# An RWKV-7 layer whose triangular inverses are turned on chip, with their lower products moved into the receptance projection

## The chip, the cores and the metric

The kernel runs on one core of one Trainium2 chip. The metric is the device time of one execution in microseconds (us), lower being better. All times below are in us unless another unit is given. The engines are TensorE (PE; its weight loads are listed as PEld), VectorE (DVE), ScalarE (ACT), GpSimd (POOL) and SyncE (SP, which here only issues DMAs).

## What is computed

Two residual layers run on 512 tokens of width 2048, in float32. Layer 0 is differential attention, and nothing of it concerns this study. Layer 1 is RWKV-7: projections to receptance r, key k, value v and gate g, a per-channel decay, and a recurrence per head of 64 channels (32 heads), followed by a normalisation per head, the gate and an output projection.

```python
p = h @ w_in                      # r, k, v, gate: 2048 columns each, and two low-rank parts
p = p + (token_shift(p) - p) * mu
...
kk = kk / max(norm(kk), 1e-12)    # per head
def step(S, inp):                 # S: 64 x 64 per head
    r_t, w_t, k_t, v_t, a_t, b_t = inp
    sa = einsum('bhvk,bhk->bhv', S, a_t)
    S = S * w_t[:, :, None, :] + sa[..., None] * b_t[:, :, None, :] + v_t[..., None] * k_t[:, :, None, :]
    y = einsum('bhvk,bhk->bhv', S, r_t)
    return S, y
```

Here a_t is -kk, and b_t is kk times a learned rate.

## The kernel before

**Pairs and chunks.** Layer 1 works through 16 pairs of heads, j = 0 to 15, of 128 channels each. The 512 steps of the recurrence are cut into eight chunks of 64. Within a chunk the recurrence is a triangular system, so the kernel computes for each chunk and head the inverse of a unit lower triangular 64x64 matrix, and with it runs a scan over eight chunks in place of 512 steps.

**Projections.** A projection of one pair (`unit_chan`) is 48 matmuls of 128x512 into the tile pp (L129): 16 slices of the 2048 inputs, each with three products. ACT casts the weights to a high part (wh, L115), and DVE subtracts to get the low part (wl, L116). Both have four buffers, so these two engines keep a little ahead of TensorE. Pair by pair the order is v(j), k(j+1), gate(j-3), r(j+1); the first three pairs have no gate.

**One pair's way.** After r(j), `stage2` completes the tile AR. Behind the 18th matmul of v(j), `gram` multiplies BK by AR per chunk and head (tile gp, L1091). ACT copies the result to G (L1098), and two matmuls (L1010, L1011) sum k squared per head, for the norm. The two 32x32 diagonal blocks of each triangular matrix (16 per half, 32 in all) go by six DMAs on ACT's queue to DRAM (ltd), and come back by four DMAs on POOL's queue as LT, one matrix per partition and repeated four times, so that each group of 32 partitions solves a quarter of the columns. `t_solve` then runs 31 steps on DVE, each with one L1155 (tmpl) and one L1157 (Tm), and a product with the norm (L1158). POOL's queue writes Tm to DRAM (td), and four DMAs on SP's queue read it into TT, the inverse's diagonal blocks. DVE transposes the upper ones into T1 (L1181). The lower left block of the inverse is minus a product of three: TensorE multiplies G's lower block by T1 (px, L1187, 16 matmuls of 32x32), ACT copies to X (L1190), TensorE multiplies X by TT's lower blocks (px, L1197), and ACT copies into TT (L1200). Both px groups do one head's eight chunks first and the other's behind them.

**The scan.** `scan_pair` does per chunk: sm<-VS,G (L1268); ACT copies to rhs (L1271); sm<-rhs,TT (L1279); ACT copies to VS (L1281); sm<-VS,BKT (L1286); DVE makes the next state (L1290). POOL's copies L1274 and L1277 stand beside it. `others` hangs transposes on TensorE at given chunks: keys (L1130) at 0 and 1, values (L1222) at 2, the finished y of pair j-2 (L1347) at 3. After the last chunk come the outputs Y (L1308, L1312) and their centring.

**What sets the order.** The scan is a generator (`Chain`) that counts projection matmuls: `tick` steps it when as many have passed as its last `yield` said. `t_combine` is the first part of the same chain. Its first step runs with the previous pair's gram, and the px groups follow after GAP_D 18 and GAP_X 19 matmuls; the scan's steps follow after GAP_T 8 with gaps (6, 8) in full pairs, (4, 5) or (3, 4) in the others. The solve has a higher scheduling priority than the scan, and the scan a higher one than the weights. Decays, queries and keys of pair j+1 (`stage1`, L1040 to L1062: the prefix l, its middle m, the exponentials E, and BK) are hung behind the scan's state steps.

Of the kernel before, what the change touches and what calls it, by code (L numbers as in the profile page):

```python
# [23 lines left out]
P = 128  # L24
# [178 lines left out]
def load_rows(g, pieces, rows, queue=None, t=None):  # L203
# [693 lines left out]
def unit_chan(g, parts, cols, step=P, more=None, behind=(0, None), pts=None):  # L897

    nc = g.nc
    n = cols // step  # L900
    pts = pts or [g.pp.tile([P, 512], F32, name="pp", tag="pp") for _ in range(n)]
    KG = 8 if cols == P else 4
    m = None
    for k0 in range(0, KT, KG):
        wh, wl = split_w(g, parts, KG, cols, k0)
        for k, c in [(k, c) for k in range(KG) for c in range(n)]:
            s = slice(c * step, (c + 1) * step)
            kk = k0 + k
            if more and c == 0:
# [3 lines left out]
            if n == 1 and 3 * kk + 3 == behind[0]:  # L913
                behind[1](m)
    return pts
# [12 lines left out]
C = 64  # L928
# [8 lines left out]
def rwkv_consts(g, aps):  # L937
# [10 lines left out]
    pb = load_rows(g, pbs, 112, t=tb)  # L948
# [28 lines left out]
def rwkv_masks(g):  # L977
# [102 lines left out]
def gram(g, j, p, before):  # L1080
# [3 lines left out]
    p.BKT = w.tile([P, NC_, P], F32, name="BKT", tag="BKT", bufs=2)  # L1084
# [8 lines left out]
    if before:  # L1093
        with g.tc.issue_after(m.ins):
            before.step(g)
    for c0, gp in halves:
        for h in range(2):
            nc.scalar.copy(p.G[:, c0 : c0 + 4, :, h, :], gp[h][:].rearrange("p (u x t) -> p u x t", u=4, x=2))  # L1098
    ps = g.ps.tile([P, 512], F32, name="pt", tag="pb", bufs=2)
    sum_channels(g, ps[:2, :], g.ones[:, 0 : P : C], p.k2)  # L1100
    ss = w.tile([2, T], F32, name="ssl", tag="thg", bufs=1)
    nc.scalar.copy(ss[:], ps[:2, :])
    for half in range(2):
        nc.scalar.dma_start(
            out=g.ltd[j % 2, half, :, :, HALF, :],
            in_=ss[:].rearrange("h (c b t) -> h c b t", c=NC_, b=2)[:, :, half, :])
    for half in range(2):
        for h in range(2):
            q0 = h * C + half * HALF
            nc.scalar.dma_start(  # L1110
                out=g.ltd[j % 2, half, h, :, 0:HALF].rearrange("c s t -> s c t"),
                in_=p.G[q0 : q0 + HALF, :, 0, h, half * HALF : (half + 1) * HALF])
# [22 lines left out]
def t_solve(g, j, p):  # L1135
# [4 lines left out]
    LT = w.tile([P, HALF + 1, HALF], F32, name="LT", tag="LT", bufs=1)  # L1140
# [4 lines left out]
    n2 = LT[:, HALF, :]  # L1145
    nc.vector.tensor_scalar(n2, n2, 1e-24, None, ALU.max)
    nc.vector.reciprocal(n2, n2)
    nc.gpsimd.memset(Tm[:], 0.0)
    tf = Tm[:].rearrange("p q t -> p (q t)")
    for i in range(NG):  # L1150
        nc.gpsimd.memset(tf[i * 32 : i * 32 + 32, i :: HALF + NG], 1.0)
# [7 lines left out]
    nc.gpsimd.dma_start(out=g.td[j % 2].rearrange("q l t -> l q t"), in_=Tm[:])  # L1159
    return ld.ins  # L1160


GAP_D, GAP_X, GAP_T = 18, 19, 8


def t_combine(g, j, p):

    nc, w, TT = g.nc, g.work, g.TT[j % 2]
    for h in range(2):
        for half in range(2):  # L1170
            o, l0 = half * HALF, half * 16 + h * NC_
            nc.sync.dma_start(
                out=TT[h * C + o : h * C + o + HALF, :, h, o : o + HALF],
                in_=g.td[j % 2].rearrange("q (g l) t -> (q g) l t", g=NG)[:, l0 : l0 + NC_, :])
    T1 = w.tile([P, NC_, HALF], F32, name="T1", tag="T1", bufs=1)
    X = w.tile([P, NC_, HALF], F32, name="X", tag="X", bufs=1)
    px = g.ps.tile([P, 512], F32, name="px", tag="pd", bufs=1)
    for h in range(2):
        r_ = slice(h * C, h * C + C)
        with g.tc.issue_after(g.centred) if g.centred else ExitStack():  # L1180
            nc.vector.transpose(T1[r_], TT[r_, :, h, 0:HALF])  # L1181
    yield GAP_D
    N = NC_ * HALF
    blocks = [(h, h * C, slice(h * C, h * C + HALF), slice(h * C + HALF, h * C + C)) for h in range(2)]
    for h, b0, lo, hi in blocks:
        for c in range(NC_):
            nc.tensor.matmul(px[hi, c * HALF : (c + 1) * HALF], p.G[lo, c, 0, h, HALF:C], T1[lo, c, :],  # L1187
                             start=True, stop=True, tile_position=(b0, b0 + HALF))
    for _, _, _, hi in blocks:
        nc.scalar.copy(X[hi], px[hi, :N].rearrange("p (c s) -> p c s", c=NC_))  # L1190
    for h, b0, _, _ in blocks:
        r_ = slice(b0, b0 + C)
        nc.scalar.copy(p.G[r_, :, 0, h, :], p.AR[r_, :, 0, :])
    yield GAP_X
    for h, b0, lo, hi in blocks:
        for c in range(NC_):
            nc.tensor.matmul(px[lo, N + c * HALF : N + (c + 1) * HALF], X[hi, c, :], TT[hi, c, h, HALF:C],  # L1197
                             start=True, stop=True, tile_position=(b0 + HALF, b0))
    for h, b0, lo, _ in blocks:
        nc.scalar.copy(TT[lo, :, h, HALF:C], px[lo, N:].rearrange("p (c s) -> p c s", c=NC_))  # L1200
    yield GAP_T
# [46 lines left out]
def chain(g, j, p, delay, gap, gap_s, others=()):  # L1248
    def steps():
        yield from t_combine(g, j, p)  # L1250
# [65 lines left out]
def centre(g, p):  # L1316
# [4 lines left out]
    for h in range(2):  # L1321
# [3 lines left out]
        c = nc.vector.tensor_sub(p.yc[:, h::2, :], yg, s1[:, :, h : h + 1].to_broadcast([P, NT, C]))  # L1325
    g.centred = c.ins
# [25 lines left out]
def layer1(g, aps):  # L1352
    nc, tc = g.nc, g.tc
    with ExitStack() as cx:
# [18 lines left out]
        def receptances(j):  # L1373
            return shift_mix(g, proj(0, j), P, *mus(g, 0, j), "r", 1)
# [3 lines left out]
        for j in range(D // P):  # L1378
            p = pairs[j]
            if j:  # L1380
                others = [(0, lambda p=p: turn_keys(g, p, 0)), (1, lambda p=p: turn_keys(g, p, 4)),
                          (2, lambda p=p: turn_values(g, p))]
                if j > 1:
                    others.append((3, lambda i=j - 2: finish_y(g, i, pairs[i])))
                full = LAG <= j < D // P - 1
                gaps = (6, 8) if full else (4, 5) if j > 1 else (3, 4)
                chain(g, j - 1, pairs[j - 1], 5, *gaps, others).step(g)
                if j == 1:
                    pairs[0].chain.wait += 28
            stage2(g, j, r, p)  # L1390

            def behind(m, j=j, p=p):
                if j > 1:
                    pairs[j - 2].chain.finish(g)
                with tc.issue_after(m.ins):
                    gram(g, j, p, j > 1 and pairs[j - 1].chain)
                mask_gram(g, p, 0)
                loaded = t_solve(g, j, p)
                with tc.issue_after(loaded):
                    mask_gram(g, p, 1)  # L1400
# [3 lines left out]
            stage_v(g, j, p, proj(2, j, behind=(18, behind)))  # L1404
# [10 lines left out]
        chain(g, j, p, 66, 5, 6)  # L1415
# [10 lines left out]
        gts.append(gate(g, j, proj(3, j, behind=(24, last_but_one)), "E"))  # L1426
# [66 lines left out]
def body(ctx, tc, nc, aps):  # L1493
    g = Ctx()
    g.nc, g.tc = nc, tc
    g.last, g.first, g.centred = None, [], None
# [11 lines left out]
    g.ltd = dr.tile([2, 2, 2, NC_, HALF + 1, HALF], F32, name="ltd")  # L1508
    g.td = dr.tile([2, HALF // NG, P, HALF], F32, name="td")
# [27 lines left out]
```

## Time and profile before

| | us |
|---|---|
| device time, median of 3 runs | 2198.23 |
| lowest and highest run | 2197.27, 2201.91 |
| profiled execution, first to last instruction (span) | 2193.6 |
| TensorE busy in it | 2161.4 |
| DVE busy | 1469.2 |
| ACT busy | 1095.1 |
| POOL busy | 302.0 |
| mean granted TensorE clock | 0.997 |

The profile gives no separate device time for the profiled execution; its span is 4.6 below the median of the runs, and that much lies around the first and last instruction. In the rows below, a group line has line, engine, operation, output and inputs, shape, count, then busy time and mean ns of one, then the idle time of the engine ahead of them and what ended it. A window row has the stretch in us from the start, its length, the busy time and count of each engine, the granted clock (1.00 is full speed), the DMA engines' busy share and GB/s. A wait row has the engine and line that waited, what it waited for, and the total, number and longest. One TensorE matmul of 32-bit data appears as two records.

### The profile page before, as it was taken

To read this page: it belongs to the slowest core of one execution; us is meant where nothing else is said; L and a number is where in the kernel's file an instruction comes from. 1 tells how busy PE (TensorE), PEld (TensorE's weight loads), DVE (VectorE), ACT (ScalarE), POOL (GpSimd) and SP (SyncE) were. 2 spreads that over 40 slices of the span, in tenths; PEclk is the share of its full clock that TensorE was granted. 3 is DMA by queue.
4 is the path that set the end of the run, shared out by engine and by line. 5 is a ranking of instruction groups with operands and counts; after the bars stand their busy time and mean duration, and the time that the engine had idled before them with its cause. 6 is when DMAs were issued, how large, how long until landed. Compare 5 with 4: busy or idle time off the path is not lost.

```text
span 2193.6 us, 35117 instructions
## 1 busy us (share of the span) xinstructions
PE 2161.4 (99%) x12260; PEld 1766.8 (81%) x12260; DVE 1469.2 (67%) x4121; ACT 1095.1 (50%) x2459; POOL 302.0 (14%) x637
## 2 busy tenths in 40 slices
PE   9999999999999999999999999999999999999999
PEld 8888888888888878878777788887888888777887
DVE  5665646465665667476667877777778877767645
ACT  6443434344443454345455566555555566555433
POOL 0000000000000000110223222222222222221001
PEclk9999999999999999999999999999999999999999
DMA  7323222222222356553422333333333333455556
GB/s 193 96 80 99 85 96 97 87 97 87 93 81 97 128 170 231 149 131 89 101 60 73 90 89 85 94 98 92 92 82 90 94 92 79 105 132 188 173 166 122
DMA packets 296321, 240.26 MB, mean 110 GB/s; under 512 B 47792, under 2 KB 255680, under 8 KB 296144
## 3 DMA queue, kind: packets, MB, share of 16 engines
q1 hardware_dynamic: 256912, 190.13, 29.3%
q0 software_dynamic: 12384, 29.72, 6.4%
q10 hardware_dynamic: 26848, 18.18, 2.7%
q8 instruction: 96, 1.57, 0.3%
q14 instruction: 81, 0.66, 0.1%
HBM read 217.98 MB, written 19.99 MB: 108 GB/s over the span
## 4 chain that ended last, share of the span: by engine, by line
PE 80%; DVE 12%; DMA 3%; ACT 3%; issue 2%; POOL 0%; ACTq 0%; DVEq 0%; SPq 0%; POOLq 0%
PE pp L129 60%; PE pt L129 5%; DVE tmpl L1155 2%; DVE wl L116 2%; DVE Tm L1157 1%; PE gp L1091 1%; PE sm L1268 1%; DMA yr<-yd 1%; PE o L129 1%; PE sc L129 1%; DMA td<-Tm 1%; PE sm L1286 1%; PE lora L129 1%; PE sm L1279 1%; DMA TT<-td 1%
## 5 line engine op out<-in xcount | busy, mean ns | idle before, releaser
L116 DVE TENSOR_TENSOR wl<-wraw,wh 128x512 fp32r<-128x512 f32 (+1 forms) x636 | 436.3, 689 | 442.2 <-ACT wh L115 429.7
L115 ACT CAST wh<-wraw 128x512 fp32r<-128x512 f32 (+1 forms) x636 | 393.3, 620 | 589.7 <-PE pp L129 484.4
L129 PE MATMUL pp<-wh,hH 128*128 128x512 f32 x1268 | 499.8, 394 | 0.6 <-DVE prmin_rw_mu_dram L210 0.6
L129 PE MATMUL pp<-wh,hL 128*128 128x512 f32 x1268 | 497.5, 393 | 0.0
L129 PE MATMUL pp<-wl,hH 128*128 128x512 f32 x1268 | 497.4, 392 | 0.0
L129 PE MATMUL pp<-hH,wl 128*128 128x512 f32 x1024 | 414.9, 405 | 0.0
L129 PE MATMUL pp<-hL,wh 128*128 128x512 f32 x1024 | 414.9, 405 | 0.0
L129 PE MATMUL pp<-hH,wh 128*128 128x512 f32 x1024 | 410.8, 401 | 0.0
L129 PEld LDWEIGHTS pp<-wh,hH 128*128 128x128 f32 x1268 | 238.3, 188 | 48.6 <-issue 1.3
L129 PEld LDWEIGHTS pp<-wh,hL 128*128 128x128 f32 x1268 | 238.3, 188 | 48.2
L129 PEld LDWEIGHTS pp<-wl,hH 128*128 128x128 f32 x1268 | 238.3, 188 | 47.1
L129 PEld LDWEIGHTS pp<-hH,wh 128*128 128x128 f32 x1024 | 193.9, 189 | 35.3 <-issue 0.9
L129 PEld LDWEIGHTS pp<-hL,wh 128*128 128x128 f32 x1024 | 193.9, 189 | 34.8
L129 PEld LDWEIGHTS pp<-hH,wl 128*128 128x128 f32 x1024 | 194.0, 189 | 32.4
L1155 DVE SCALAR_TENSOR_TENSOR tmpl<-LT,Tm 128x60 f32<-128x60 f32 (+24 forms) x496 | 133.9, 270 | 11.2
L1274 POOL COPY SA<-VS 64x64 f32<-64x64 f32 x224 | 62.0, 277 | 443.3 <-DVE VS L1290 361.7
L476 POOL DMA_DIRECT2D frow<-yd x12 | 8.9, 746 | 795.9 <-DVE rs_t L67 675.6
L1157 DVE TENSOR_TENSOR Tm<-Tm,tmpl 128x60 f32<-128x60 f32 (+24 forms) x496 | 102.4, 206 | 8.1
L1281 ACT COPY VS<-sm 64x64 f32<-64x64 f32 x256 | 52.9, 207 | 60.5 <-PE sm L1279 50.9
L1271 ACT COPY rhs<-sm 64x64 f32<-64x64 f32 x256 | 52.7, 206 | 60.5 <-PE sm L1268 56.6
L1277 POOL TENSOR_SCALAR Sg<-SA,gam 128x64 f32<-128x64 f32 x96 | 70.2, 731 | 9.5
L1290 DVE SCALAR_TENSOR_TENSOR VS<-sm,gam,Sg 64x64 f32<-64x64 f32 x192 | 54.1, 282 | 19.4 <-PE sm L1286 14.4
(333 smaller groups left out, 3197.9 us busy)
## 6 DMA issues: line engine op xcount, KB each, us to landing
wraw<-in_rw_w_in_dram SPq DMA_DIRECT2D x128, 512.0 KB
wraw<-in_da_w_in_dram SPq DMA_DIRECT2D x254, 256.0 KB
wraw<-in_da_w_out_dram SPq DMA_DIRECT2D x26, 512.0 KB
wraw<-in_rw_w_out_dram SPq DMA_DIRECT2D x26, 512.0 KB
LT<-ltd POOLq DMA_DIRECT2D x64, 132.0 KB, 3.0
yr<-yd SPq DMA_DIRECT2D x28, 256.0 KB
frow<-yd POOLq DMA_DIRECT2D x12, 512.0 KB, 6.5
xq<-in_x_dram SPq DMA_DIRECT2D x16, 256.0 KB
```

Source lines behind the costliest of these rows:

```text
L115: nc.scalar.copy(hi[:], raw[:, k : k + n])
L116: nc.vector.tensor_sub(lo[:], raw[:, k : k + n], hi[:].bitcast(F32))
L129: m = nc.tensor.matmul(out, a, b, start=s, stop=e, skip_group_check=skip)
L1091: m = nc.tensor.matmul(gp[h][:, i * P : (i + 1) * P], BK[r_, c0 + i, :, :], p.AR[r_, c0 + i, :, :], start=True, stop=True)
L1155: nc.vector.scalar_tensor_tensor(tt, LT[:, i : i + 1, i + 1 :].to_broadcast([P, s, n]), n2[:, i : i + 1], Tm[:, 0:s, i : i + 1].to_broadca ...
L1157: nc.vector.tensor_add(Tm[:, 0:s, i + 1 :], Tm[:, 0:s, i + 1 :], tt)
L1268: nc.tensor.matmul(sm[:, 0:P], both(p.G[:, c, 0]), both(VS[:, c]), start=True, stop=True)
L1271: nc.scalar.copy(rhs[r_, :], sm[r_, h * C : h * C + C])
L1274: nc.gpsimd.tensor_copy(p.SA[r_, c - 1, :], VS[r_, c, h, :])
L1277: nc.gpsimd.tensor_scalar(Sg[:], p.SA[:, c - 1, :], p.gam[:, c : c + 1], None, ALU.mult)
L1281: nc.scalar.copy(VS[r_, c, h, :], sm[r_, P : P + C])
L1290: g.state = nc.vector.scalar_tensor_tensor(VS[r_, c + 1, h, :], s_, p.gam[r_, c : c + 1], Sg[r_, :], ALU.mult, ALU.add)
```

## The change

The inverse's blocks no longer pass through DRAM, and the lower products and the norms are put in other places.

- ACT copies the diagonal blocks of G to a tile LP (four copies of 32x256), and one transpose on DVE makes LT from it, four times repeated. Tm starts as a copy of a constant (`unit`), made by POOL once. After the 31 steps and the product, two transposes on DVE make T1 and W, and POOL copies W into TT's diagonal blocks. The tiles ltd and td are gone.
- The norms are summed in the receptance projection of the same pair, behind its 24th matmul (`norms`), and three DMAs on POOL's queue take them through a small DRAM tile nd to n2.
- The px groups of pair j-1 become `t_first` and `t_second`, behind the 9th and 33rd matmul of r(j), with the two heads alternating. Only for the last pair do they still run in the chain (`whole`).
- The scan's chain of pair j-1 starts with r(j) done, after 3 matmuls, with gaps (7, 8) in full pairs, (5, 6) for j below 3 and (4, 5) for j = 15. The transposes of values move from chunk 2 to 4, those of y from 3 to 5.
- Both halves of the mask on G are issued before the solve. The order of T1 behind the centring is gone. One parameter tile moves from the const pool to a temporary one.

```diff
 def gram(g, j, p):
...
+    p.LP = w.tile([P, NC_, HALF], F32, name="LP", tag="tmpl", bufs=1)
+    for h in range(2):
+        for half in range(2):
+            q = slice(h * C + half * HALF, h * C + half * HALF + HALF)
+            nc.scalar.copy(p.LP[q], p.G[q, :, 0, h, half * HALF : (half + 1) * HALF])
+def norms(g, j, p, m):
...
+    with g.tc.issue_after(m.ins):
+        sum_channels(g, ps[:2, :], g.ones[:, 0 : P : C], p.k2)
...
 def t_solve(g, j, p):
...
+    nc.vector.transpose(LT[:].rearrange("p (r c) t -> p t r c", r=NG),
+                        p.LP[:].rearrange("p c t -> p t c")[:, :, None, :].to_broadcast([P, HALF, NG, NC_]))
...
-    for i in range(NG):
-        ld = nc.gpsimd.dma_start(out=LT[i * 32 : i * 32 + 32], in_=g.ltd[j % 2].rearrange("b h c s t -> (b h c) s t"))
...
+    nc.gpsimd.tensor_copy(Tm[:], g.unit[:])
...
-    nc.gpsimd.dma_start(out=g.td[j % 2].rearrange("q l t -> l q t"), in_=Tm[:])
...
+    nc.vector.transpose(p.T1[:].rearrange("p c (q r) -> p q r c", r=NG),
+                        Tm[:].rearrange("p q (r c) -> p q r c", r=NG))
+    p.W = w.tile([P, NC_, HALF], F32, name="W", tag="Tm", bufs=1)
+    nc.vector.transpose(p.W[:], p.T1[:])
...
+            nc.gpsimd.tensor_copy(g.TT[j % 2][q, :, h, o : o + HALF], p.W[q])
...
+def t_first(g, j, p):
...
+    for c in range(NC_):
+        for h, b0, lo, hi in BLOCKS:
+            nc.tensor.matmul(px[hi, c * HALF : (c + 1) * HALF], p.G[lo, c, 0, h, HALF:C], p.T1[lo, c, :],
                              start=True, stop=True, tile_position=(b0, b0 + HALF))
...
+def t_second(g, j, p):
...
+    for c in range(NC_):
+        for h, b0, lo, hi in BLOCKS:
+            nc.tensor.matmul(px[lo, N + c * HALF : N + (c + 1) * HALF], p.X[hi, c, :], p.W[hi, c, :],
                              start=True, stop=True, tile_position=(b0 + HALF, b0))
...
+            behind = [(24, lambda m: norms(g, j, pairs[j], m))]
+            if j:
+                behind += [(9, piece(t_first, j - 1, pairs[j - 1])), (33, piece(t_second, j - 1, pairs[j - 1]))]
+            return shift_mix(g, proj(0, j, behind=behind), P, *mus(g, 0, j), "r", 1)
...
-                gaps = (6, 8) if full else (4, 5) if j > 1 else (3, 4)
-                chain(g, j - 1, pairs[j - 1], 5, *gaps, others).step(g)
-                if j == 1:
-                    pairs[0].chain.wait += 28
+                gaps = (7, 8) if full else (5, 6) if j < LAG else (4, 5)
+                chain(g, j - 1, pairs[j - 1], 3, *gaps, others)
```

Three places show how the order moves. The first is TensorE in a full pair. Before, around the gram in v(j), the px groups stand together beside the gram (G and T are those of pair j-1, gp and the sums pt those of pair j):

```order
L129 MATMUL pp<-hL,wh 128x512
L129 MATMUL pp<-hH,wl 128x512
L1187 MATMUL px<-T_14796,G_14131 32x32 x8
L1091 MATMUL gp<-AR,BK 128x128 x2
L1187 MATMUL px<-T_14796,G_14131 32x32 x8
L1091 MATMUL gp<-AR,BK 128x128 x14
L1197 MATMUL px<-TT_10025,X 32x32 x16
L1010 MATMUL pt<-sHx,ones 2x512
L1011 MATMUL pt<-sLx,ones 2x512
L129 MATMUL pp<-hH,wh 128x512
```

Now, in r(j), the second px group stands behind the outputs of the pair before and the norms' sums, and the first stands 24 projection matmuls ahead of it, alone (not in these rows):

```order
L129 MATMUL pp<-hH,wl 128x512
L1328 MATMUL Y<-VS,G_14881 64x64 x16
L1332 MATMUL Y<-SA,AR 64x64 x14
L1019 MATMUL pt<-sHx,ones 2x512
L1020 MATMUL pt<-sLx,ones 2x512
L129 MATMUL pp<-hH,wh 128x512
L129 MATMUL pp<-hL,wh 128x512
L129 MATMUL pp<-hH,wl 128x512
L129 MATMUL pp<-hH,wh 128x512
L129 MATMUL pp<-hL,wh 128x512
L129 MATMUL pp<-hH,wl 128x512
L1211 MATMUL px<-W,X 32x32 x16
```

So px left v, and the gram stands there without it. The second place is ACT in the k projection, where the scan's rhs and VS of one pair meet the decays (m, l, E) and BK of the next. Before:

```order
L1054 ACTIVATE BK<-th_15229,prm_bk_b_1234,prm_bk_s_1231 128x8x64
L1271 COPY rhs<-sm 64x64 x2
L115 CAST wh<-wraw 128x512
L1044 ACTIVATE E<-m 128x8
L1045 ACTIVATE E<-l 128x8x64
L1281 COPY VS<-sm 64x64 x2
L1046 ACTIVATE l<-l 128x512
```

Now:

```order
L115 CAST wh<-wraw 128x512
L1053 ACTIVATE E<-m 128x8
L1063 ACTIVATE BK<-th_15215,prm_bk_b_1233,prm_bk_s_1230 128x8x64
L1291 COPY rhs<-sm 64x64 x2
L1054 ACTIVATE E<-l 128x8x64
L1055 ACTIVATE l<-l 128x512
L1301 COPY VS<-sm 64x64 x2
```

E<-m moved ahead of rhs. What it reads comes from DVE, whose rows at the same place were, before, in the middle of the solve:

```order
L1157 TENSOR_TENSOR Tm<-Tm,tmpl 128x3x22
L1040 SCALAR_TENSOR_TENSOR l<-rmask,th_15223 128x512
L1155 SCALAR_TENSOR_TENSOR tmpl<-LT,Tm 128x63
L1042 TENSOR_SCALAR m<-l 128x8
L1157 TENSOR_TENSOR Tm<-Tm,tmpl 128x3x21
L1043 TENSOR_TENSOR l<-l,m 128x512
L1155 SCALAR_TENSOR_TENSOR tmpl<-LT,Tm 128x60
```

And now:

```order
L1169 SCALAR_TENSOR_TENSOR tmpl<-LT,n_15449,Tm 128x8
L1049 SCALAR_TENSOR_TENSOR l<-rmask,th_15926 128x512
L1171 TENSOR_TENSOR Tm<-Tm,tmpl 128x8
L1051 TENSOR_SCALAR m<-l 128x8
L1172 TENSOR_TENSOR Tm<-Tm,n_15449 128x256
L1052 TENSOR_TENSOR l<-l,m 128x512
L1174 STREAM_TRANSPOSE T_15702<-Tm 128x32x8
```

The scan for l and m moved from the solve's 11th step to its last, because the solve starts earlier against the projections.

The third place is TensorE at pair 0, in r(1), where the built order puts t_first behind 31 projection matmuls of r(1), and the norms' sums and t_second right behind it:

```order
L129 MATMUL pp<-hH,wh 128x512
L1196 MATMUL px<-T_10382,G_10278 32x32 x16
L1019 MATMUL pt<-sHx,ones 2x512
L129 MATMUL pp<-hL,wh 128x512
L129 MATMUL pp<-hH,wl 128x512
L129 MATMUL pp<-hH,wh 128x512
L129 MATMUL pp<-hL,wh 128x512
L129 MATMUL pp<-hH,wl 128x512
L1211 MATMUL px<-W,X 32x32 x16
L129 MATMUL pp<-hH,wh 128x512
```

In the order before, r(1) holds no px; px of pair 0 comes in v(1), beside the gram.

More of the change, by code (lines that the diff above doesn't have):

```diff
@@ L912, in unit_chan @@
                     kk == 0, kk == KT - 1, g)
-            if n == 1 and 3 * kk + 3 == behind[0]:
-                behind[1](m)
+            for at, follow in behind:
+                if 3 * kk + 3 == at:
+                    follow(m)
     return pts
@@ L1177, in t_combine @@
[L1177 to L1182, printed above, removed]
+            o = half * HALF
+            q = slice(h * C + o, h * C + o + HALF)
+            nc.gpsimd.tensor_copy(g.TT[j % 2][q, :, h, o : o + HALF], p.W[q])
+BLOCKS = [(h, h * C, slice(h * C, h * C + HALF), slice(h * C + HALF, h * C + C)) for h in range(2)]
@@ L1495, in body @@
     g.nc, g.tc = nc, tc
[L1496 removed]
+    g.last, g.first = None, []
     g.chains, g.later, g.state = [], [], None
```

128 lines of the change are left out of this document (61 added, 67 removed).

## Prediction

> **What bounds the kernel now.** I read the page's engine totals and its chain first, then the stretches from one gram (L1091) to the next, then what TensorE waits for. The first two lines come from the page.
>
> ```profile
> PE 2161.4 (99%) x12260; PEld 1766.8 (81%) x12260; DVE 1469.2 (67%) x4121; ACT 1095.1 (50%) x2459; POOL 302.0 (14%) x637
> PE 80%; DVE 12%; DMA 3%; ACT 3%; issue 2%; POOL 0%; ACTq 0%; DVEq 0%; SPq 0%; POOLq 0%
> ```
>
> TensorE is busy nearly always, so an edit pays only where it shortens TensorE's own work or one of its few stops. Layer 0 keeps its order. Layer 1 I cut at the gram's start: the first row is pair 0's gram to pair 1's, then pairs 1, 2 and 3, ten pairs in one row, pair 14, and the rest. After the range and its length come the busy times of PE, PEld, DVE, ACT and POOL, the granted clock and the DMAs.
>
> ```profile
> 1038.13:1076.98 38.85, 38.84 (x200) 31.51 (x199) 24.32 (x63) 21.96 (x41) 5.90 (x10) 1.00 0.36 90
> 1076.98:1140.59 63.61, 57.96 (x369) 44.13 (x368) 44.38 (x136) 31.76 (x79) 15.81 (x36) 0.89 0.30 75
> 1140.59:1196.33 55.74, 53.54 (x374) 39.89 (x373) 41.80 (x133) 32.43 (x80) 17.52 (x36) 1.00 0.27 67
> 1196.33:1263.29 66.96, 64.03 (x453) 49.70 (x452) 51.71 (x154) 36.31 (x87) 17.52 (x42) 1.00 0.37 95
> 1263.29:1877.92 614.63, 607.95 (x4187) 497.35 (x4185) 474.38 (x1379) 358.77 (x860) 159.46 (x360) 1.00 0.35 90
> 1877.92:1941.46 63.54, 61.59 (x440) 50.38 (x437) 48.32 (x139) 36.22 (x86) 15.95 (x36) 1.00 0.44 118
> 1941.46:2193.60 252.14, 246.73 (x1325) 198.19 (x1322) 153.68 (x333) 106.74 (x225) 40.38 (x67) 1.00 0.56 157
> ```
>
> A steady pair takes 614.63/10 = 61.46. Pairs 1 and 2 lack a gate projection, 48 matmuls. The chain gives their price:
>
> ```profile
> 1062.08 14.96 PE pp L129 x66
> ```
>
> That is 0.2267 each, so 10.9 for 48, and pairs 1 and 2 should take about 50.5. Pair 1 is 13.1 over, pair 2 is 5.2, pair 3 is 5.5, pair 14 is 2.1. That excess is what there is to win. Its cause is in the waits of PE, and for pair 1 in the chain and in windows around the longest wait:
>
> ```profile
> PE px L1187 <- DVE T L1181: 10.4, 9, 4.5
> PE sm L1268 <- DVE VS L1290: 4.8, 14, 0.6
> PE sm L1279 <- ACT rhs L1271: 1.1, 2, 0.7
> ```
>
> ```profile
> 1087.57 0.43 DVE Tm L1158
> 1088.29 3.23 DMA td<-Tm
> 1091.67 1.74 DMA TT<-td
> 1093.43 0.45 DVE T L1181
> ```
>
> ```profile
> 1089.00:1093.90 4.90, 0.39 (x2) 0.00 (x0) 1.93 (x5) 0.59 (x1) 2.04 (x9) 0.92 0.52 126
> 1093.90:1106.30 12.40, 12.38 (x86) 9.63 (x86) 2.37 (x4) 3.72 (x9) 2.68 (x4) 0.50 0.48 111
> 1203.70:1206.20 2.50, 0.96 (x6) 0.48 (x4) 0.43 (x2) 0.59 (x1) 0.75 (x5) 1.00 0.30 48
> ```
>
> At px of pair 0, TensorE stood 4.5 for the inverse's way through DRAM, and then ran 12.4 at half clock, which lost about 6 more. The stop in pair 3 (2.50 − 0.96, about 1.5) did not do that: pair 3's whole stretch has 1.00.
>
> **The change, part by part.** *Early pairs.* The way from Tm to T1 (1087.57 to 1093.88, 6.3) becomes Tm's product and one transpose, about 0.9, and the loading of LT through DRAM becomes four copies on ACT and a transpose on DVE. But px of pair 0 now stands behind the 31st matmul of r(1), some 25 earlier. TensorE gets there at about 1062.1 − 0.5 (the norms' two sums have moved) + 31 × 0.2267 = 1068.6. The other side of that race:
>
> ```profile
> 1039.32 2.05 ACT L1098 COPY G<-gp 128x512 f32<-128x512 f32 x4 [2.05 <-PE gp L1091]
> 1059.08 0.24 DVE L1155 SCALAR_TENSOR_TENSOR tmpl<-LT,Tm 128x31 f32<-128x31 f32 x1
> L115 ACT CAST wh<-wraw 128x512 fp32r<-128x512 f32 x160 | 99.3, 621 | 112.5 <-PE pp L129 97.3 <-issue 14.2
> L1200 ACT COPY TT<-px 32x256 f32<-32x256 f32 x20 | 7.3, 365 | 0.1
> L1181 DVE STREAM_TRANSPOSE T<-TT 64x256 f32<-64x256 f32 x19 | 8.3, 439 | 5.2 <-DMA TT<-td 4.9
> ```
>
> G is copied at 1041.4; four LP copies at the row of L1200 and one cast make it 1043.5. LT's transpose has no row. It makes 1024 numbers per partition where T1's makes 256. Bounds: 0.44 (one T1) and 3.5 (eight, if the 64 partitions per row also count); I take 1.3, on the side of its nearest row times the fourfold width (1.76), less a start cost shared once. The solve took 28.5 before (1059.08 to 1087.57); with the LT transpose ahead and less idling I get T1 at 1070 to 1073.6. So TensorE waits 1.5 to 5 there; I take 3.0. Into this first interval move px of pair 0 (2.3 by the rows below) and, by the order, seven small blocks of its scan, some 0.2 each like the two gram matmuls between the px halves (0.42): 3.7. With the packing's saving, 1.0, the interval changes by 3.7 − 1.0 + 3.0 = **+5.7**.
>
> Pairs 1 and 2 then lose their excess but for such waits as pair 2 shows apart from TensorE's work, 55.74 − 53.54 = 2.2: 50.5 + 0.2 − 1.0 + 2.2 = 51.9 each, so **−11.7 and −3.8**. Bounds for each are 49.7 (no wait) and 54.7 (pair 2's whole excess stays). Pair 3 goes to the steady pair below, 61.0: **−6.0**. Pair 14 likewise: **−2.5**; its 63.54 holds half a px group more than a steady pair and 1.95 without TensorE's work.
>
> *px with alternating heads.* This is TensorE's own work, in all 16 pairs.
>
> ```profile
> 1631.14 0.69 PE L1187 MATMUL px<-T,G 32*32 32x32 f32 x16
> 1631.76 0.49 PE L1091 MATMUL gp<-AR,BK 64*128 64x128 f32 x4
> 1634.56 1.09 PE L1197 MATMUL px<-TT,X 32*32 32x32 f32 x32
> 1635.58 0.40 PE L1010 MATMUL pt<-sHx,ones 128*2 128x512 f32 x1
> 1139.09 0.68 PE L1312 MATMUL Y<-SA,AR 64*64 64x64 f32 x28
> 1139.70 0.50 PE L129 MATMUL pp<-hH,wh 128*128 128x512 f32 x1
> ```
>
> A group of 32 px records takes 1.24 in two halves (1631.14 to 1631.76, twice) or 1.02 in one (1634.56 to 1635.58): 32 ns a record, one head after the other. L1312, whose heads alternate, needs 22 ns a record (0.61 for 28). Within L1197 alone, two windows of 0.16, the second at the point where the first head's records end:
>
> ```profile
> 1634.72:1634.88 0.16, 0.16 (x10) 0.16 (x9) 1.00 0.00 0
> 1635.04:1635.20 0.16, 0.16 (x14) 0.16 (x11) 1.00 0.00 0
> ```
>
> In the second the heads meet, and 14 records are under way instead of 10, so two heads run beside each other. At 16 ns a group takes 0.51. Bounds are nothing and the whole halving, 1.1 per pair; I take 1.05. It hides nowhere: TensorE is the bound. The Trainium skill speaks against it: "TensorEngine Tiling (Array Packing)", Restrictions and Gotchas, says that different row tiles write different PSUM banks and cannot use one bank at once, and here both heads write px. By that rule the 32 ns would stay and the sum below would be 17 higher; the second window, with 14 records under way, disagrees.
>
> *A steady pair.* Gone is TensorE's wait for T1, 2.0 in ten pairs by the last figure of its group there:
>
> ```profile
> L1187 PE MATMUL px<-T,G 32*32 32x32 f32 x307 | 13.3, 192 | 2.2 <-DVE T L1181 2.0
> ```
>
> The px groups stand apart now, one interruption more; by the 0.50 of the first matmul after L1312 it costs 0.1 on each of two matmuls, 0.2. New is a wait of TensorE for rhs. ACT now has E<-m and a BK ahead of the fifth rhs of the scan; before, rhs stood ahead of E:
>
> ```profile
> 1602.50 0.42 ACT L1271 COPY rhs<-sm 64x64 f32<-64x64 f32 x2
> 1603.47 0.21 ACT L1044 ACTIVATE E<-m 128x8 f32<-128x8 f32 x1
> 1604.07 0.64 ACT L1045 ACTIVATE E<-l 128x512 f32<-128x512 f32 x1 [0.39 <-DVE l L1043]
> L1054 ACT ACTIVATE BK<-th,prm_bk_b,prm_bk_s 128x512 f32<-128x512 f32 x20 | 15.2, 812 | 0.0
> 1593.83 0.25 DVE L1155 SCALAR_TENSOR_TENSOR tmpl<-LT,Tm 128x31 f32<-128x31 f32 x1
> 1624.20 0.42 DVE L1158 TENSOR_TENSOR Tm<-Tm,LT 128x256 f32<-128x256 f32 x1
> ```
>
> And m now stands at the solve's last step (before: at step 11 of 31). From the gram's end, ACT copies G (1.35 left), LP (1.46), one cast and one rhs (1.04): LT can start at 3.85. From LT to m the order has 31 steps, six weight subtractions, eight state updates, two mixes, one product and the scan, 26 by the mean durations of before. There, the 94 DVE instructions between the last two rows have durations that sum to 33.3 and took 30.37, 0.91 of it. So m comes at 27.6 (0.91) to 29.9 (1.0), and rhs 1.4 later, past E, BK and itself: 29.0 to 31.4. TensorE has 102 projection matmuls (23.2) and some 6.4 of other blocks between gram and the matmul on rhs, so it asks at about 29.6. The wait is 0 to 1.8; I take 0.6. What queues behind on ACT are rhs, E and the next casts, and TensorE waits for these. Sum: 61.46 − 0.2 + 0.2 − 1.05 + 0.6 = 61.0, over ten pairs **−4.5**.
>
> Costed at nothing: POOL's copies of the unit, of W into TT and the norms' three DMAs (POOL is busy 16 of 61 per pair, and its results are wanted half a projection later; a late TT would stop the scan's first matmul on it), ACT's six and SP's four DMA issues, the const tile moved.
>
> *Tail.* px's second group of pair 14 and some scan steps left it (2.3), and pair 15's px saves 1.05: **−3.3**.
>
> **Sum:** +5.7 − 11.7 − 3.8 − 6.0 − 4.5 − 2.5 − 3.3 = −26.1. Span 2193.6 becomes 2167.5. The median of the runs is 2198.2, 4.6 above the span, which I add: 2172.
>
> **Rivals.** *No packing.* Two heads that write one bank go one after the other. For it speaks that no px group of before alternates, so that no row has the price; against it stands the second of the two windows. Then 16 × 1.05 = 17 comes back: 2189. The tiling page of the Trainium skill stands for this outcome.
>
> *Half clock once more.* If the wait at px of pair 0 is 4.5 rather than 3.0, TensorE runs at half speed for some 12.4 again, as at 1093.90: +1.5 + 6 gives 2179. The wait of about 1.5 did not do it, so the point lies between. "TensorE: Matmul & The Clock Gate", Part 1, in the Trainium skill, puts it at about 3.4 idle; the two stops agree with that.
>
> *DVE's queue is late (slower).* All of the solve's transposing falls on DVE, whose 47.4 of 61.5 per pair becomes over 49, and the prefix m stands at its end. If LT takes 3.5 and the instructions run at their plain sum, m is 2.2 + 1.8 later than the 0.91 case and ACT holds rhs for 3.5 to 4 in each of twelve pairs. That gives +2.9 × 12 = 35 or a little more over the forecast: about 2207. It decides from a wait of 2.8 per pair, where the whole gain of 26 is eaten. Against it: pairs before ran at 0.91 with DVE full.
>
> *The stops only move.* Earlier placing gives the scan of the early pairs the same waits elsewhere, and packing and new waits cancel: about 2198.
>
> **How the numbers follow.** Forecast 0.54, no packing 0.14, half clock 0.09, DVE late 0.17, stops move 0.06. A measurement here cannot tell less than 0.2%, 4.4, from no change. Faster by more: 0.54 + 0.09 + most of no packing and a little of the last, 0.75; within: 0.07; slower: 0.18. The forecast alone spans 2160 to 2184 by its bounds (early wait 1.5 to 5, pairs 1 and 2, rhs 0 to 1.8). The range to 2204 takes in no packing and the cheaper part of the late DVE; its low end has no new wait and no wait in pairs 1 and 2, 2158.
>
> **What would show it.** px groups of 32 records in 0.5 to 0.6 (right) or 1.0 (no packing). LT's transpose near 1.3. One stop of 1.5 to 5 at the first px, with a clock of 1.00 behind it. Steps of 61 from gram to gram, and a wait of TensorE for rhs under 1 per pair. Wrong: waits for rhs or VS above 2 in every pair, or pairs 1 and 2 still near 55.

## The result, and the profile after

The changed kernel takes 2201.18 us (median of 20 runs, 2198.94 to 2205.72), the kernel before 2200.10 (20 runs on the same chip, 2196.27 to 2209.91). The ratio is 1.0005, with a 95% interval of 0.9997 to 1.0012: no difference that can be told, where 2172 was forecast. The profiled execution has a span of 2197.2, against 2193.6 before and 2167.5 forecast. So 29.7 us of the forecast are missing.

The page's engine totals and chain shares, of the changed kernel:

```profile
PE 2143.5 (98%) x12260; PEld 1751.9 (80%) x12260; DVE 1522.4 (69%) x4137; ACT 1122.5 (51%) x2523; POOL 327.9 (15%) x614
PE 74%; DVE 17%; ACT 5%; issue 3%; DMA 1%; ACTq 0%; DVEq 0%
```

TensorE's busy time fell by 18 while its span grew: its work got shorter, and it stands still for longer. By the clock of 0.89 over the 63.6 of pair 1, nearly 7 of the 18 is the half clock that is gone. On the chain, DMA went from 3% to 1%, and DVE came from 12% to 17% and ACT from 3% to 5%. The stretches from gram to gram, cut as before (pair 0, 1, 2, 3, ten full pairs, pair 14, the rest):

```profile
1039.64:1085.44 45.80, 41.68 (x273) 33.78 (x273) 37.57 (x100) 27.62 (x56) 10.59 (x17) 1.00 0.28 75
1085.44:1137.50 52.06, 49.33 (x369) 38.87 (x369) 43.02 (x121) 33.77 (x84) 18.14 (x35) 1.00 0.24 64
1137.50:1189.96 52.46, 49.51 (x374) 39.49 (x373) 45.90 (x133) 33.32 (x84) 17.44 (x34) 1.00 0.24 64
1189.96:1253.20 63.24, 60.83 (x422) 49.11 (x421) 50.75 (x140) 37.68 (x91) 17.05 (x35) 1.00 0.27 74
1253.20:1885.42 632.22, 608.35 (x4201) 491.15 (x4200) 507.21 (x1391) 376.78 (x901) 170.19 (x341) 1.00 0.27 74
1885.42:1949.61 64.19, 61.34 (x424) 49.27 (x423) 51.13 (x141) 37.86 (x91) 18.07 (x37) 1.00 0.35 98
1949.61:2197.20 247.59, 241.28 (x1277) 195.45 (x1276) 154.60 (x326) 103.47 (x216) 40.95 (x64) 1.00 0.55 155
```

| stretch | before | forecast | after |
|---|---|---|---|
| gram of pair 0, start | 1038.1 | 1038.1 | 1039.6 |
| pair 0 | 38.9 | 44.6 | 45.8 |
| pairs 1, 2 | 63.6, 55.7 | 51.9, 51.9 | 52.1, 52.5 |
| pair 3 | 67.0 | 61.0 | 63.2 |
| ten pairs | 614.6 | 610.1 | 632.2 |
| pair 14 | 63.5 | 61.0 | 64.2 |
| rest | 252.1 | 248.8 | 247.6 |

Pairs 0 to 2 and the rest came out as forecast within 1.3 each. The twelve full pairs (3 to 14) take 63.2 (pair 14: 64.2) and not 61.0, which is 27.5 of the missing 29.7. That the total is just what it was before is a coincidence: up to pair 3 and in the rest 14.6 was won, and from pair 4 to 14 18.2 was lost. What TensorE waits for, in all of the changed kernel:

```profile
PE sm L1288 <- DVE VS L1310: 22.2, 40, 1.4
PE sm L1299 <- ACT rhs L1291: 11.4, 13, 0.9
PE px L1196 <- DVE T L1174: 3.8, 3, 1.9
```

The wait for T1 went from 10.4 to 3.8, its longest from 4.5 to 1.9, and the clock stays at 1.00 in every stretch of this execution (the fastest of the 20; the mean clock of the others is 0.998 to 1.000). In its place stand waits for the scan's state on DVE (4.8 before) and for rhs (1.1 before). One full pair shows both. First DVE and TensorE behind the turn of LT:

```profile
1574.14 1.50 DVE L116 TENSOR_TENSOR wl<-wraw,wh 128x512 fp32r<-128x512 f32 x1 [1.38 <-ACT wh L115]
1575.57 2.23 DVE L1158 STREAM_TRANSPOSE LT<-LP 128x1024 f32<-128x1024 f32 x1
...
1578.82 0.69 DVE L116 TENSOR_TENSOR wl<-wraw,wh 128x512 fp32r<-128x512 f32 x1
1579.43 0.25 DVE L1169 SCALAR_TENSOR_TENSOR tmpl<-LT,n,Tm 128x29 f32<-128x29 f32 x1
1579.71 0.28 DVE L1310 SCALAR_TENSOR_TENSOR VS<-sm,gam,Sg 64x64 f32<-64x64 f32 x1
```

```profile
1580.55 0.46 PE L1288 MATMUL sm<-VS,G 128*128 128x128 f32 x2 [0.79 <-DVE VS L1310]
```

The product that this state is made from was on TensorE at 1577.12 to 1577.5; DVE reaches the update at 1579.71, behind the turn, five solve instructions and a weight subtraction. The next two states cost stops of 0.37 and 0.30 in the same way. Then ACT at the end of the solve, and TensorE's matmul on rhs:

```profile
1603.00 0.22 ACT L1053 ACTIVATE E<-m 128x8 f32<-128x8 f32 x1 [0.89 <-DVE m L1051]
1603.12 0.80 ACT L1063 ACTIVATE BK<-th,prm_bk_b,prm_bk_s 128x512 f32<-128x512 f32 x1
1603.93 0.42 ACT L1291 COPY rhs<-sm 64x64 f32<-64x64 f32 x2
```

```profile
1604.41 0.43 PE L1299 MATMUL sm<-rhs,TT 128*128 128x64 f32 x2 [0.93 <-ACT rhs L1291]
```

ACT stands at E for m, with BK and rhs queued behind it: the wait that the prediction named, larger than it took. The four stops of a full pair are 0.79 + 0.37 + 0.30 + 0.93 = 2.4.

The theory to test: TensorE's own saving is real, and these stops eat it. They have two causes, a DVE that is full around LT's turn and the solve (28.3 of the 30.3 from 1574.1 to 1604.4 are busy), and ACT's E standing ahead of the scan's copies. The rivals: LT's turn alone, or POOL's masks beside it, or the places of the instructions and not DVE's load, or that alternating heads save nothing.

### The profile page after: what moved, and what is told of

Its sections match the earlier page's. It is cut to its first block, busy times and chain, and to the rows that moved or that the text cites. A ratio compares the mean times of both kernels' runs of the same rounds, so it can differ in the third digit from the quotient of the medians.

```text
span 2197.2 us, 34826 instructions
## 1 busy us (share of the span) xinstructions
PE 2143.5 (98%) x12260; PEld 1751.9 (80%) x12260; DVE 1522.4 (69%) x4137; ACT 1122.5 (51%) x2523; POOL 327.9 (15%) x614
## 4 chain that ended last, share of the span: by engine, by line
PE 74%; DVE 17%; ACT 5%; issue 3%; DMA 1%; ACTq 0%; DVEq 0%
PE pp L129 57%; PE pt L129 5%; DVE tmpl L1169 4%; DVE Tm L1171 3%; DVE wl L116 3%; DVE VS L1310 2%; ACT G L1103 1%; DVE LT L1158 1%; PE o L129 1%; PE sc L129 1%; PE lora L129 1%; PE gp L1099 1%; PE sm L1288 1%; ACT wh L115 1%; PE Y L1328 1%
## 5 line engine op out<-in xcount | busy, mean ns | idle before, releaser
L116 DVE TENSOR_TENSOR wl<-wraw,wh 128x512 fp32r<-128x512 f32 (+1 forms) x636 | 449.9, 709 | 457.2 <-ACT wh L115 441.2
L129 PE MATMUL pp<-hH,wh 128*128 128x512 f32 x1024 | 416.1, 406 | 0.0
L1294 POOL COPY SA<-VS 64x64 f32<-64x64 f32 x224 | 74.7, 334 | 478.4 <-DVE VS L1310 397.0
L1169 DVE SCALAR_TENSOR_TENSOR tmpl<-LT,n,Tm 128x60 f32<-128x60 f32 (+24 forms) x496 | 135.7, 274 | 14.6
L1291 ACT COPY rhs<-sm 64x64 f32<-64x64 f32 x256 | 52.5, 205 | 84.3 <-PE sm L1288 82.3
L1301 ACT COPY VS<-sm 64x64 f32<-64x64 f32 x256 | 52.8, 206 | 68.4 <-PE sm L1299 63.2
L1288 PEld LDWEIGHTS sm<-VS,G 128*128 128x128 f32 x256 | 43.8, 188 | 50.0 <-PE pp L129 34.8
L1288 PE MATMUL sm<-VS,G 128*128 128x128 f32 x256 | 53.3, 290 | 22.6 <-DVE VS L1310 22.2
```

Source lines behind the costliest of these rows:

```text
L116: nc.vector.tensor_sub(lo[:], raw[:, k : k + n], hi[:].bitcast(F32))
L129: m = nc.tensor.matmul(out, a, b, start=s, stop=e, skip_group_check=skip)
L1169: nc.vector.scalar_tensor_tensor(tt, LT[:, i : i + 1, i + 1 :].to_broadcast([P, s, n]), n2[:, i : i + 1], Tm[:, 0:s, i : i + 1].to_broadca ...
L1288: nc.tensor.matmul(sm[:, 0:P], both(p.G[:, c, 0]), both(VS[:, c]), start=True, stop=True)
L1291: nc.scalar.copy(rhs[r_, :], sm[r_, h * C : h * C + C])
L1294: nc.gpsimd.tensor_copy(p.SA[r_, c - 1, :], VS[r_, c, h, :])
```

## The experiments

All ratios are to the kernel before, run on the same chip. Line numbers of an experiment's rows are its own.

| run | median | ratio, 95% interval |
|---|---|---|
| e1 thin turn (leaves work out) | 2195.05 | 0.9971 (0.9961 to 0.9982) |
| e2 masks later | 2244.84 | 1.0198 (1.0184 to 1.0212) |
| e3 rhs ahead of E | 2202.98 | 1.0010 (1.0001 to 1.0019) |
| e4 before, heads alternating | 2194.38 | 0.9968 (0.9956 to 0.9981) |
| e5 heads in turn | 2213.95 | 1.0053 (1.0037 to 1.0070) |
| e6 E behind VS | 2188.26 | 0.9937 (0.9920 to 0.9954) |
| e7 state ahead of the solve | 2198.75 | 0.9991 (0.9980 to 1.0001) |
| e8 e6 and e7 | 2189.61 | 0.9943 (0.9924 to 0.9963) |
| e9 e6 and gaps (6, 10) | 2178.53 | 0.9892 (0.9869 to 0.9916) |
| e10 e6 and gaps (7, 10) | 2188.51 | 0.9941 (0.9920 to 0.9962) |
| e11 gaps (6, 10) alone | 2203.18 | 1.0008 (0.9997 to 1.0019) |
| e12 e9, scan 8 later | 2287.51 | 1.0386 (1.0367 to 1.0404) |
| e13 e9 and thin turn (leaves work out) | 2167.80 | 0.9844 (0.9826 to 0.9862) |
| e14 e9, scan 3 later | 2188.29 | 0.9947 (0.9928 to 0.9966) |
| e14 e9, scan 5 later | 2198.51 | 0.9993 (0.9983 to 1.0004) |

**Does the alternation save TensorE's time?** e4 is the kernel before with the loops of its px groups exchanged, e5 the changed kernel with them exchanged back.

```diff
-    for h, b0, lo, hi in blocks:
-        for c in range(NC_):
+    for c in range(NC_):
+        for h, b0, lo, hi in blocks:
```

> The kernel before with the two heads alternating in its px groups and nothing else. Theory A (alternating heads run beside each other even in one bank): each group falls from 1.02 to 1.24 down to about 0.62, 1.0 per pair, 16 pairs: 2183 to 2186. Rival (px is shorter in the changed kernel because it stands alone there): 2198 to 2202.

> The changed kernel with its px groups one head after the other, as before the change. Theory A (alternating heads save TensorE's own time in r, where nothing else stops it): each group goes from 0.62 back to 1.02 or more, 0.8 to 1.0 per pair, 16 pairs: 2214 to 2217. Rival (the saving is eaten by waits that end at the same time anyway, as in the kernel before): 2200 to 2206.

In the changed kernel a group takes 0.62 from start to start (32 records, 19 ns each):

```profile
1613.80 0.69 PE L1196 MATMUL px<-T,G 32*32 32x32 f32 x32
1614.42 0.50 PE L129 MATMUL pp<-hH,wh 128*128 128x512 f32 x1
```

e5's full pair takes 64.0 and not 63.2, and its time is 11 (by the ratios) to 13 (by the medians) above the changed kernel's: most of the saving, as forecast. e4 gains 7 only. Its ten full pairs take as long as before (613.7 against 614.6), since the earlier px only waits longer for T1 (first row, of e4; 10.4 before), and the norms' sums behind it for G (second row):

```profile
PE px L1187 <- DVE T L1181: 15.7, 14, 4.8
PE pt L1010 <- ACT G L1098: 2.8, 10, 0.3
```

So the same edit is worth most of its price where px waits for nothing, and little where it does. Before the change the full pairs too were held by the solve.

**Is it LT's turn alone, or the masks?** e1 turns 8 of LT's 32 columns and leaves the rest at zero. e2 puts POOL's masks behind the turn.

```diff
-    nc.vector.transpose(LT[:].rearrange("p (r c) t -> p t r c", r=NG),
-                        p.LP[:].rearrange("p c t -> p t c")[:, :, None, :].to_broadcast([P, HALF, NG, NC_]))
+    nc.vector.transpose(LT[:].rearrange("p (r c) t -> p t r c", r=NG)[:, :8],
+                        p.LP[:].rearrange("p c t -> p t c")[:, :8, None, :].to_broadcast([P, 8, NG, NC_]))
```

> The changed kernel with LT turned for 8 of its 32 columns only, into a tile set to zero once; the other columns are left out, so DVE's turn of LT is a quarter of 2.23 us, about 0.6. Theory A (the turn on DVE makes DVE's queue late, and TensorE waits for VS behind it, 0.79 + 0.37 + 0.30 per full pair, and for rhs, 0.93): all these waits go, 12 pairs x 2.2 to 2.4, so 2172 to 2176. Theory B (the waits come from where scan, E and px now stand, and DVE's load does not matter): within 4 of the changed kernel, 2197 to 2203.

> The changed kernel with POOL's four masks on G held behind LT's turn by a small copy that reads LT. Theory P (the masks run beside DVE's weight subtraction and LT's turn and stretch them: 1.51 for a subtraction that usually takes 0.69, and 2.23 for the turn): the subtraction falls to 0.7 and the turn to about 1.4, the waits of the full pairs lose 0.8 to 1.0 each, 2189 to 2192. Theory A (the turn takes 2.2 by its size, four times the 0.61 of T1's): the turn stays at 2.1 to 2.3, the time at 2198 to 2203.

e1 came out between the two: 6 less by the medians (its profiled execution is the slowest of its runs, 2198.99). Its waits of TensorE show why:

```profile
PE sm L1308 <- ACT VS L1303: 12.5, 14, 1.0
PE sm L1290 <- DVE VS L1312: 11.9, 33, 1.0
```

The waits for the state halve (22.2 to 11.9), and the stop behind E stays as large as it was: it now holds the copy VS in place of rhs. E follows the state update of the scan's fifth chunk wherever that is. Theory A as written falls, since the turn is one of two causes.

e2 shows that the masks do not lengthen the turn, but do lengthen what has two inputs. The groups of e2, ten full pairs:

```profile
L116 DVE TENSOR_TENSOR wl<-wraw,wh 128x512 fp32r<-128x512 f32 x160 | 111.5, 697 | 95.1 <-ACT wh L115 87.2 <-PE sm L1302 7.8
L1158 DVE STREAM_TRANSPOSE LT<-LP 128x1024 f32<-128x1024 f32 x10 | 22.3, 2231 | 4.7 <-ACT LP L1108 4.7
```

The turn stays at 2.23, and the subtraction's mean falls from 750 ns to 697. Yet the time grew by 44, because the masks now run beside the solve. Of the 27 that its ten full pairs lose, about half is half clock behind the longer stops (mean clock 0.98). DVE in e2, right behind the turn, where POOL has masks from 1604.69 to 1608.9:

```profile
1604.61 0.25 DVE L1171 SCALAR_TENSOR_TENSOR tmpl<-LT,n,Tm 128x31 f32<-128x31 f32 x1
1604.90 0.53 DVE L1173 TENSOR_TENSOR Tm<-Tm,tmpl 128x31 f32<-128x31 f32 x1
1605.46 1.08 DVE L1171 SCALAR_TENSOR_TENSOR tmpl<-LT,n,Tm 128x30 f32<-128x30 f32 x1
...
1607.78 1.13 DVE L1171 SCALAR_TENSOR_TENSOR tmpl<-LT,n,Tm 128x29 f32<-128x29 f32 x1
1608.94 0.28 DVE L1313 SCALAR_TENSOR_TENSOR VS<-sm,gam,Sg 64x64 f32<-64x64 f32 x1
```

A step of 0.25 takes up to 1.13, the state comes at 1608.94, and TensorE stands 3.07. The place of the masks ahead of the solve, which the change gave them, is worth keeping.

**Is it E's place?** e3 issues ACT's exponentials behind the next rhs, e6 behind the next VS copy. The rows are e6's; e3 does the same with the copy to rhs.

```diff
+        if g.turn and g.exps:
+            with g.tc.issue_after(g.turn.ins):
+                g.exps.pop()()
...
-            nc.scalar.copy(VS[r_, c, h, :], sm[r_, P : P + C])
+            g.turn = nc.scalar.copy(VS[r_, c, h, :], sm[r_, P : P + C])
```

> The changed kernel with ACT's exponentials (E<-m, E<-l, l, f) issued behind the next rhs instead of ahead of it. Theory A: the wait for rhs goes (0.93 in the trace and as much hidden in the row, 1.2 in all per full pair), the waits for VS stay: 2186 to 2190. Theory B2 (DVE bounds the stretch, so that a wait taken away at rhs comes back at the next VS): 2197 to 2202.

> The changed kernel with ACT's exponentials E of the next pair issued behind the next VS copy of the scan, past rhs and VS. Theory C (ACT stands at E for m and l, with the scan's copy queued behind it, whichever copy that is): the wait of 1.2 per full pair goes, the three waits for the state on DVE stay: 2184 to 2190. Theory D (DVE is so full from the turn of LT to the prefix l that the stop comes back at the next state update): 2197 to 2203.

In e3 the stop goes from rhs to the next copy, VS, as large as before (12.4 in 14 waits), and the time stays. In e6, where both copies go first, it is gone: a full pair takes 62.0, 1.2 less, and the time is 13 to 15 below the changed kernel's. What is left are the state's waits, unchanged:

```profile
PE sm L1296 <- DVE VS L1318: 22.3, 40, 1.4
```

**What are the state's stops?** e7 sets the solve's priority below the scan's (`@ahead(2500)` in place of `@ahead(SOLVE)`), e8 adds e6. e9 to e11 change the gaps.

```diff
-                gaps = (7, 8) if full else (5, 6) if j < LAG else (4, 5)
+                gaps = (6, 10) if full else (5, 6) if j < LAG else (4, 5)
```

> The changed kernel with the solve's scheduling priority below the scan's, so that DVE's two state updates come together and ahead of the solve's steps that are ready by then. Theory C: the waits for VS (1.46 per full pair as shown, 1.7 by the interval between matmuls) shrink to 0.6, the wait at rhs behind E stays: 2184 to 2190. Theory D: the solve gets later by what the state gets earlier, and TensorE waits for rhs or T1 instead: 2196 to 2204.

> The last two together. Theory C: both waits of the full pairs go, 12 x 2.3 to 2.9, and the time comes to that of the forecast: 2168 to 2176. Theory D: no more than 5 below the changed kernel, 2196 to 2203.

> The kernel of e6 (exponentials behind VS) with the scan's gaps in full pairs (6, 10) instead of (7, 8): as many projection matmuls per chunk, but two more of them (0.46) behind the product that DVE makes the state from. Theory C (TensorE waits for VS because DVE reaches the state update late by a fixed lag of 0.3 to 0.8 behind the solve's steps that stand ahead of it): the stops of 0.79, 0.37 and 0.30 fall to 0.3 and nothing, about 1.1 per pair, 2174 to 2178. Theory D (DVE is full there, so that the order of TensorE does not matter): 2185 to 2191.

> The same with gaps (7, 10): the chunk is longer by two matmuls, and the scan reaches further into r. Theory C: 2172 to 2178, as e9 or a little better, since ACT's copies keep their seven matmuls. Theory D: 2185 or more, and a later decay prefix.

> The changed kernel with gaps (6, 10) and the exponentials left ahead of rhs. Theory C: the stops for VS go as in e9, the stop at rhs behind E stays at 1.2 or grows by 0.2 because rhs is wanted one matmul earlier: 2187 to 2192. Theory D: 2198 to 2204.

e7 and e8: the new order does not help. The state's waits come to 23.9 and 22.1, and only 2.4 was won, none on top of e6. But the order moved little. The two state updates now stand together, yet the first begins 3.98 behind the start of the turn (4.14 in the changed kernel), still behind four solve instructions and a weight subtraction. An order with the state right behind the turn was not built, so what it would save is not shown. e9 is the best kernel that computes everything, 1.1% below the one before. But its waits say that the stops were gathered rather than removed: 20.1 in all, per full pair one of about 1.08 behind the turn and one of 0.22:

```profile
PE sm L1296 <- DVE VS L1318: 20.1, 28, 1.4
```

```profile
1570.48 0.46 PE L1296 MATMUL sm<-VS,G 128*128 128x128 f32 x2 [1.08 <-DVE VS L1318]
```

Of the 6.6 that its ten full pairs gain over e6's, 4.5 come from the gram (2.04 in place of 2.49, see the end). In e11 the stop behind E grows from 0.9 to 1.6 as those for the state shrink, and nothing is won. In e10 a new stop comes at VS (17.7 in 14 waits), in the third chunk and not behind E: ACT stands at y (the part of the output that comes straight from the values, L1236) for DVE, with the VS copy queued behind it:

```profile
1579.23 0.72 ACT L1236 ACTIVATE y<-y,prm_hgb 128x512 f32<-128x512 f32 x1 [3.20 <-DVE y L1235]
1579.97 0.44 ACT L1309 COPY VS<-sm 64x64 f32<-64x64 f32 x2
```

**One place, or a full DVE?** e12 and e14 begin e9's scan later (`11`, `6` or `8 if full else 3` in place of the delay `3`); e13 is e9 with e1's thin turn.

> The kernel of e9 with the scan of the full pairs begun eight projection matmuls (1.8) later, so that the state of its first chunk reaches DVE when the turn of LT is over. Theory E (what is left of the stops for VS is one stop of 1.08, the first state update behind LT's turn and the steps that follow it): the stop goes, 12 x 1.0: 2165 to 2169. Theory D (DVE is full from the turn on, and stops come back at later states or at px): 2176 to 2182.

> The kernel of e9 with the thin turn of e1 (LT turned for 8 of its 32 columns, the rest left out; 0.68 in e1 instead of 2.23). Theory E (the stop of 1.08 is the turn's length): the stop falls by 1.0 to 1.08, 2165 to 2168. Rival (the built order fills the room with more of the solve's steps, as in e1): 2173 or more.

> The kernel of e9 with the scan of the full pairs begun three projection matmuls (0.68) later, which keeps the outputs Y ahead of the second px group. Theory E (the rest is one stop, of the first state behind LT's turn): the stop falls from 1.08 to 0.4, 12 x 0.68: 2169 to 2172. Theory D: 2176 to 2181.

> The same with five projection matmuls (1.13): theory E: the stop goes, 2165 to 2169. Theory D, or a later state that comes in the stop's place: 2173 to 2181.

e13 takes 10.7 off e9, and its full pair is 60.7. The turn is 1.56 shorter there, of which 0.7 per pair arrive:

```profile
PE sm L1298 <- DVE VS L1320: 9.7, 28, 1.0
L1168 DVE STREAM_TRANSPOSE LT<-LP 128x256 f32<-128x256 f32 x10 | 6.8, 681 | 0.0
```

So with the stop at rhs gone and 0.65 per pair left at the state, a full pair takes what was forecast, 61.0, or a little less (the gram is 0.45 shorter than in the changed kernel).

Moving the scan does not help; it costs 10 to 109 over e9. With three matmuls the pair has one stop of 1.8 at a state. With five it has one of 0.4 at a state and one of 1.96 at the VS copy, again behind y, and half clock in six of the twelve pairs, which take 1.5 longer for it. e12 ended most of the stops at the state (4.9 in all) and has stops at VS instead (21.5 in 25 waits, 17.4 of it behind y). Besides, it let the outputs Y run into the second px group, and its mean clock in the ten full pairs is 0.94; a full pair takes 9 longer than in e9. So theory E, one place, holds only as far as the turn's length counts. Wherever E, the gaps and the scan were put, the stops at rhs, VS and the state that a full pair kept came to 1.3 (e9) to 2.8 (e11), as long as DVE's work stayed.

## Why the prediction was wrong, step by step

- **Early pairs: right.** 51.9 each was forecast for pairs 1 and 2, 52.1 and 52.5 were measured. TensorE stood 1.9 at the first px (3.0 was taken, with bounds of 1.5 and 5), and in the profiled execution the clock stayed at 1.00. Pair 0 took 1.2 more than forecast, with a stop of 2.3 of a values' transpose behind the solve that was not on the list.
- **Packing: right in size and mechanism.** 1.05 per pair was taken; the groups fell from 1.24 and 1.02 to 0.62 each, 1.02 per pair. e5 gives 0.8 per full pair for it. The rule of the Trainium skill, "TensorEngine Tiling (Array Packing)", Restrictions and Gotchas, by which row tiles cannot use one bank at once, does not fit these rows: 19 ns a record and not 32.
- **The turn of LT: wrong size.** 1.3 was taken, 2.23 measured, within the bounds of 0.44 to 3.5. The row used was of 64 partitions in pieces; the new T1, 128x256 in one instruction, takes 0.61, and four times that is 2.44. By e1, a quarter of the turn takes 0.68, and each further quarter 0.52.
- **The wait for rhs: right mechanism, too small.** 0.6 was taken; the stop is 0.93, and between the matmuls around L1299 1.2 is lost per pair. e6 takes it away and wins 1.2 per full pair. LT's turn begins 3.8 behind the gram's end, as computed (3.85), but m is done 31.2 behind it and not 27.6 to 29.9; 0.9 of the difference is the longer turn. The prediction let it hang on DVE's lateness alone; e1 shows that it stays when DVE is early, because E hangs behind the fifth chunk's state.
- **The step that failed: "What queues behind on ACT are rhs, E and the next casts, and TensorE waits for these."** Here the steady pair's list of new waits ended. The scan's state on DVE was not on it, and cost nothing in the sum. It costs 1.46 of standing per full pair, where it was 0.3 (between the matmuls around L1288, 1.7 more than before). The solve was checked for when it ends, not for whom it holds on the way. Before, the solve began 23.5 behind the start of its gram (1593.83 and 1570.32); now LT's turn begins 6.3 behind it (1575.57 and 1569.24), just where the state of the second chunk is due.
- **The rival "DVE's queue is late"** named the cause, and its point of decision: a wait of 2.8 per pair eats the whole gain. By the intervals between matmuls around L1288 and L1299, full pairs lose 1.7 + 1.2 = 2.9 more than before, and the gain is gone. Its place was half right: rhs as forecast, and the state besides.

The sum for a full pair, in the forecast's terms: 61.46 − 0.2 (T1) − 1.0 (packing) + 2.9 (state and rhs) + 0.3 (gram) makes 63.5, against 63.22; around L1306 TensorE loses 0.3 less than before (2.9 and 3.3). What stays open is whether DVE's stretch can be shortened without leaving work out, and what an order with the state right behind the turn would give; no version here did either.

## What to carry to other kernels

When a chain through DRAM is replaced by work on an engine, the latency that goes was also time in which that engine served others; list every instruction that will queue behind the new work, not only the last one that must be ready. A saving on the bounding engine arrives only in stretches where that engine waits for nothing (e4 against e5). And an engine that stands at an instruction for another engine holds whatever copy stands next in its order, so moving one copy past it (e3) only passes the stop on, and other instructions take the same part (y in e10).

## What the hardware showed that was not expected

- Instructions of DVE with two inputs in SBUF can run two to five times as long beside POOL's masks: a subtraction 1.50 in place of 0.69, a solve step 1.13 in place of 0.25; the transpose, with one input, takes 2.23 with and without them. The Trainium skill, "SBUF — State Buffer", Who interferes with whom, says that DVE instructions with two SBUF inputs contend with POOL instructions that read SBUF, and that those with one input, outside the two-port modes, do not. The traces agree. Not every such instruction is stretched: a subtraction at 1607.17 in e2 took 0.68, and the mask that started in the same moment took 1.70, where the other mask of its size took 1.16.
- The same small matmuls of two heads do not always run side by side alike. The gram takes 2.49 in the changed kernel, where about the first eight records come one after the other, mostly 110 ns apart, and 2.04 in e9, where all come 52 to 59 ns apart but for one interval near the start. In the gram before, the two heads' records start 6 to 7 ns apart, then 105 ns to the next two. What decides between these was not tested:

```profile
1632.46 2.56 PE L1099 MATMUL gp<-AR,BK 64*128 64x128 f32 x32
```

```profile
1559.30 2.11 PE L1107 MATMUL gp<-AR,BK 64*128 64x128 f32 x32
```

- Matmuls of two different tile shapes in turn are dear. In e12, where Y (128x64) and px (32x32) alternate two by two, a pair of records takes 0.26 and 0.17, at full clock; in blocks of one kind they need 35 and 19 ns a record:

```profile
1594.40 0.33 PE L1336 MATMUL Y<-VS,G 128*64 128x64 f32 x2
1594.66 0.24 PE L1219 MATMUL px<-W,X 32*32 32x32 f32 x2
1594.83 0.33 PE L1336 MATMUL Y<-VS,G 128*64 128x64 f32 x2
```

- The length of a stop alone does not say whether half clock follows. In e2, the same stop of 3.07 to 3.09 in each full pair was followed by half clock in nine of twelve. The first row is behind such a stop, the second behind another:

```profile
1610.26:1613.67 3.41, 3.41 (x9) 2.64 (x9) 3.17 (x11) 1.10 (x3) 0.25 (x1) 0.50 0.00 0
1410.03:1414.00 3.97, 3.97 (x20) 3.35 (x21) 3.66 (x13) 1.51 (x5) 0.63 (x2) 1.00 0.00 2
```

In e14 with five matmuls, a stop of 1.95 was enough in six pairs of twelve, well below the 3.4 that the prediction quotes; again one of each:

```profile
1334.92:1338.33 3.41, 3.41 (x10) 2.64 (x9) 2.61 (x11) 0.62 (x1) 0.91 (x3) 0.50 0.00 0
1398.84:1402.25 3.41, 3.41 (x18) 2.80 (x17) 3.24 (x12) 1.03 (x3) 0.91 (x3) 1.00 0.00 0
```

And in e12 half clock came in every full pair behind the alternating Y and px, where TensorE did not stand at all:

```profile
1594.30:1600.30 6.00, 6.00 (x56) 4.43 (x56) 0.00 (x0) 0.32 (x1) 1.16 (x2) 1.00 0.66 175
1600.34:1607.16 6.82, 6.82 (x48) 5.40 (x49) 2.91 (x8) 1.90 (x4) 1.21 (x4) 0.50 0.02 2
```

In the profiled execution of the changed kernel, the stops of 2.3 and 1.9 left the clock at 1.00.
